# Ten conditioning pieces summed by VectorE instead of TensorE, in a two-block transformer kernel, with weight buffers given back one at a time

## The chip, the cores and the metric

The kernel runs as one program on 1 core of a Trainium2 chip. The metric is the device time of one execution in microseconds; before the change it was 2329.08 us (median of 3 runs, 2328.78 to 2331.86). The core's engines work side by side, each through its own instructions in order: TensorE (PE; PEld are its weight loads), VectorE (DVE), ScalarE (ACT), GpSimd (POOL), and SyncE (SP), which here only issues the DMAs.

## The reference, cut to what matters

Two blocks of two layers each work on 256 latent and 256 context tokens of width 1024, in fp32. Each layer is steered by adaLN parameters, a vector times a wide weight matrix, once for the latent and once for the context condition:

```
# first block, layer i
mod_lat = (silu_c @ ada_w[i] + ada_b[i])[:, None, :]      # 3 x 1024
mod_ctx = silu_cc @ ada_w[i] + ada_b[i]
# second block, layer l
sh1, sc1, g1, sh2, sc2, g2 = adaln_params(c, w_mod[l], b_mod[l])        # 6 x 1024
csh1, csc1, cg1, csh2, csc2, cg2 = adaln_params(c_ctx, w_mod[l], b_mod[l])
...
x = x + g2 * conv_ffn(hf, w_up[l], conv_w[l], w_down[l])
if not last:                      # the last layer leaves the context tokens out
    xc = xc + cg2 * conv_ffn(hcf, w_up[l], conv_w[l], w_down[l])
```

The first block has an HGRN2 layer (16 heads) and an MLA layer (16 heads); each layer of the second block has a mixer (attention, pooling, Fourier) and a conv-FFN. In the last layer of each block some of the six (or three) parameters are used for the latent tokens alone: the gate of the MLA layer, and all but the first shift and scale of the second block's layer 1.

## The kernel before, in words

**Stages.** The first block's HGRN2 layer (L0) runs to about 835 us of the span, its MLA layer (L1) to about 1120, the second block's layer 0 to about 1910, with its FFN from about 1490, and layer 1 to the end. All activations stay in SBUF; weights are streamed from HBM once.

**Products.** An fp32 product is made of three fp32r products: a matrix is split into a high part (a cast, `hi`, by ScalarE) and a low part (`lo = raw - hi`, by VectorE), and `mm3` issues hi times hi, hi times lo and lo times hi. Each weight is split so when it arrives.

**Weight stream.** `plan` lists all chunks of weights in the order of use; a chunk is at most 128 x 1024 fp32 (512 KB). `load_chunk` issues its DMA on SP's queue into one of `RAW = 3` buffers (`wraw`), `weights_hi` and `weights_lo` split it into one of `HL = 4` pairs of buffers (`whi`, `wlo`). The raw buffer is free after the low part is made, and its next DMA is issued then; the pair is free when the whole work item that used it is done:

```
for r in it.run(w):
    ...
freed[0] += it.n
```

**Order.** Work items stand in strings written by hand (`L0_ORDER`, `L1_ORDER`, `MIX1`, `MIX2`, `FFN`); in `FFN`, `v` and `g` are up products (one chunk each), `d` and `e` the two down products (each 9 items; an item has one chunk of two row blocks, `d5` and `d7` half a chunk, `d8` four chunks), and `A` takes the next adaLN item. Chains of small operations (norms, attention heads, evictions) run as generators between the items; a clock kept while the program is built decides where their instructions go.

**adaLN pieces.** A piece is 512 columns of one parameter matrix; it has four items (256 rows, one chunk). `ada_one` multiplies both conditions at once: the stationary tile `condc` holds four columns (latent and context, hi and lo), the moving tile the weight's hi and lo parts, four matmuls of 512 columns per item. `fin` then copies the 4 x 512 result, transposes it with four small matmuls and adds the bias. In all there are 36 pieces.

**Masks.** `k_lvl` (level masks of HGRN2) and `k_band` (window mask) come as fp32 and VectorE casts them to bytes.

**L1's first items.** `c` projects keys and values of all four token tiles (2, 3, 0, 1), `a` the queries, `z` gates, `q` and `k` open a group of heads.

Of the kernel before, what the change touches and what calls it, by code (L numbers as in the profile page):

```python
# [29 lines left out]
def shape_constants():  # L30
# [11 lines left out]
    c["k_lvl"] = m  # L42
# [12 lines left out]
    c["k_band"] = np.stack([bad[0:128, 128:256], bad[128:256, 0:128]], 1).astype(f32)  # L55
# [26 lines left out]
def tile_two_blocks(ctx: ExitStack, tc: tile.TileContext, I, out: bass.AP):  # L82
# [48 lines left out]
    def note(kind, op, a, k):  # L131
# [22 lines left out]
        "c a z1 q0 k0 z0 z2 q1 k1 z3 o1 x q2 k2 o0 z5 q3 k3 z4 o2 o3 z6 z7 o4 o5 o6 o7")  # L154
# [5 lines left out]
    MIX2 = (  # L160
        "A A a0 A g02 g03 a2 g04 A g05 a4 g06 g07 a6",
        "a0 g03 g02 a2 g04 g07 A g05 a4 g06 a6 A")
    FFN = (
# [150 lines left out]
    plan, loaded, raws, parts_of = [], [], {}, {}  # L314
    freed = [0]
# [7 lines left out]
    n_first = 16  # L323

    def place(name, dt, j, n_set, n):
        if j < n_first:
            return first_pool[0].tile([P, 1024], dt, tag="s" + name, name="s" + name, bufs=n_set)
        return wp.tile([P, 1024], dt, tag="w" + name, name="w" + name, bufs=n)

    def load_chunks(j, after):  # L330

        while len(loaded) < len(plan) and (len(loaded) <= j + SRAW if len(loaded) < n_first
                                           else len(loaded) <= max(j, n_first - 1) + RAW):
            load_chunk(len(loaded), after)

    def load_chunk(j, after):
        loaded.append(j)
        raw = place("raw", F32, j, SRAW, RAW)
# [8 lines left out]
    def weights_hi():  # L347
        for j, (parts, fn, need) in enumerate(plan):
            yield cond(lambda: j in raws and j < freed[0] + (HL if j >= n_first else SHL))
# [4 lines left out]
            if isinstance(fn, tuple):  # L354
                parts_of[j] = fn[0](raw)
            else:
                m, n = raw.shape[1], fn or parts[0].shape[1]
                hi = place("hi", F32R, j, SHL, HL)
                act.copy(hi[:, :m], raw)
                parts_of[j] = hi[:, :m], n  # L360
            tell(("whi", j))

    def weights_lo():
        for j, (parts, fn, need) in enumerate(plan):
            yield has(("whi", j))
            raw = raws.pop(j)
            if isinstance(fn, tuple):
                parts_of[j] = fn[1](raw, parts_of[j])
            else:
                hi, n = parts_of[j]  # L370
                m = hi.shape[1]
                lo = place("lo", F32R, j, SHL, HL)
# [3 lines left out]
            load_chunks(j, last[0])  # L376

    class Item:
# [4 lines left out]
        def __init__(self, run, chunks=(), need=None, first=None):  # L383
            self.run, self.need, self.chunks, self.start = run, need, chunks, first or len(chunks)

    def register(items):

        for it in items:
            it.first, it.n = len(plan), len(it.chunks)
            plan.extend(c if isinstance(c, tuple) else (c, None, None) for c in it.chunks)  # L390

    def run_items(items):
        for it in items:
            if it.need is not None:
                until(it.need)
            w = []
# [7 lines left out]
            last[0] = 0.0  # L404
# [7 lines left out]
            freed[0] += it.n  # L412
# [8 lines left out]
    def mm3(ps, ops, start=True, stop=True, every=0):  # L421
# [80 lines left out]

    def cond_split(cname, ccname):

        st = const.tile([P, KD, 4], F32R, tag="cond" + cname, name="cond" + cname)
        for j, nm in enumerate((cname, ccname)):
            sg = small("cs_s", 8)
# [18 lines left out]
    def ada_one(w, cname, bias, b0, mname, j, k2):  # L526
# [4 lines left out]
        def fin():  # L531
            r = sp.tile([4, 512], F32, tag="ada_r", name="ada_r", bufs=1)
# [1506 lines left out]
```

## Time and profile before

| | value |
|---|---|
| median of 3 runs | 2329.08 us |
| time of the profiled execution | 2327.35 us |
| its span (first to last instruction) | 2325.3 us |
| mean granted TensorE clock | 0.984 of full speed |
| busy: TensorE | 2225.0 us (96%) |
| busy: VectorE | 1669.0 us (72%) |
| busy: ScalarE | 1124.3 us (48%) |
| DMA, mean over the span | 125 GB/s, 290.63 MB |

Busy time is the union of an engine's instructions. A matmul's own duration is longer than the distance to the next one, since they overlap in the array; what a matmul costs is read from the distance between starts. A row's bracket says how long the engine had been idle before it and what ended that.

### The profile page before, as it was taken

The page shows a single profiled execution, that of the slowest core. Times are in us where ns is not written, and L with a number is a line of the kernel's source. Part 1 is how long each engine was busy: PE and PEld are TensorE (multiplying, and loading weights), DVE is VectorE, ACT ScalarE, POOL GpSimd, SP SyncE. Part 2 cuts the span into 40 slices and gives each one's busy share as a digit, 9 for nine tenths or more (in the row PEclk, how much of TensorE's full clock was granted, in tenths as well). Part 3 has the DMA queues.
Part 4 walks back from the last instruction along what each step waited for, and adds up shares of the span by engine and source line. Part 5 has one row for each costly group of instructions (what it writes and reads, how often), then busy time and mean ns, then how long its engine had stood idle before and what let it go on. Part 6 is the DMA issues. An engine that isn't in the chain of part 4 may idle for free.

```text
span 2325.3 us, 33917 instructions
## 1 busy us (share of the span) xinstructions
PE 2225.0 (96%) x13051; PEld 1893.0 (81%) x13051; DVE 1669.0 (72%) x3016; ACT 1124.3 (48%) x1963; POOL 35.8 (2%) x38
## 2 busy tenths in 40 slices
PE   5999999999999987999899999999999999998998
PEld 3888888888888877889788878876777878997987
DVE  6677867776778777888757854688746646876977
ACT  7344444443445345565445533466523335655644
POOL 0000000000000000000000000100010010000000
PEclk8999999999999998999999999999999999998999
DMA  7223324332434223233422344267643234455664
GB/s 254 68 73 110 108 91 119 99 109 91 127 100 127 92 91 90 81 106 126 147 83 90 100 136 127 64 208 217 207 156 109 91 93 127 136 164 153 195 192 140
DMA packets 324043, 290.63 MB, mean 125 GB/s; under 512 B 10562, under 2 KB 257706, under 8 KB 323882
## 3 DMA queue, kind: packets, MB, share of 16 engines
q1 hardware_dynamic: 323881, 288.47, 40.3%
q8 instruction: 103, 1.69, 0.3%
q14 instruction: 59, 0.48, 0.1%
HBM read 287.34 MB, written 1.09 MB: 124 GB/s over the span
## 4 chain that ended last, share of the span: by engine, by line
PE 86%; DVE 6%; ACT 2%; DMA 2%; issue 1%; SPq 0%; DVEq 0%; ACTq 0%
PE psmm L195 64%; PE pssm L195 19%; PE pssm L201 3%; DVE wlo L180 2%; ACT whi L180 1%; DMA wraw<-in_w_mod_dram 0%; DMA wraw<-in_w_in_dram 0%; DVE x L180 0%; DMA wraw<-in_w_out_dram 0%; ACT pssm L180 0%; DVE rs_t L180 0%; DVE PT L180 0%; DMA wraw<-in_w_down_dram 0%; DVE b_st L180 0%; DVE rt L180 0%
## 5 line engine op out<-in xcount | busy, mean ns | idle before, releaser
L180 DVE TENSOR_TENSOR wlo<-wraw,whi 128x1024 fp32r<-128x1024 f32 (+1 forms) x504 | 607.8, 1218 | 185.2 <-ACT whi L180 178.9
L180 ACT CAST whi<-wraw 128x1024 fp32r<-128x1024 f32 (+1 forms) x504 | 519.3, 1040 | 388.8 <-PE psmm L195 275.1
L195 PE MATMUL psmm<-hhi,whi 128*128 128x512 f32 (+1 forms) x1832 | 651.0, 355 | 4.8 <-ACT hhi L180 2.3
L195 PE MATMUL psmm<-hhi,wlo 128*128 128x512 f32 (+1 forms) x1832 | 634.5, 346 | 13.1 <-DVE wlo L180 13.1
L195 PE MATMUL psmm<-hlo,whi 128*128 128x512 f32 (+1 forms) x1832 | 633.1, 346 | 5.0 <-DVE hlo L180 5.0
L195 PEld LDWEIGHTS psmm<-hhi,wlo 128*128 128x128 f32 x1832 | 350.4, 191 | 58.3 <-DVE wlo L180 15.3
L195 PEld LDWEIGHTS psmm<-hhi,whi 128*128 128x128 f32 x1832 | 350.5, 191 | 48.5 <-ACT whi L180 3.1
L195 PEld LDWEIGHTS psmm<-hlo,whi 128*128 128x128 f32 x1832 | 350.0, 191 | 42.2 <-DVE hlo L180 5.8
L180 DVE TENSOR_TENSOR X<-X,Tn 128x512 f32<-128x512 f32 x192 | 123.9, 687 | 56.6 <-PE pssm L195 29.0
L195 PE MATMUL psmm<-whi,yh 128*128 128x512 f32 x412 | 163.7, 397 | 0.4 <-ACT yh L180 0.4
L195 PE MATMUL psmm<-wlo,yh 128*128 128x512 f32 x412 | 160.8, 390 | 0.1
L195 PE MATMUL psmm<-whi,yl 128*128 128x512 f32 x412 | 160.7, 390 | 0.0
L195 PE MATMUL psmm<-wlo,hhi 128*128 128x256 f32 x464 | 132.9, 286 | 5.4 <-DVE wlo L180 5.4
L195 PE MATMUL psmm<-whi,hhi 128*128 128x256 f32 x464 | 136.8, 295 | 1.3 <-ACT hhi L180 1.3
L195 PE MATMUL psmm<-whi,hlo 128*128 128x256 f32 x464 | 132.7, 286 | 0.3 <-DVE hlo L180 0.2
L195 PE MATMUL pssm<-X,Km 128*128 128x128 f32 x896 | 126.7, 285 | 1.3 <-ACT Km L180 1.3
L180 ACT COPY Km<-X 128x512 f32<-128x512 f32 x112 | 74.4, 665 | 108.4 <-DVE X L180 73.7
L195 PEld LDWEIGHTS pssm<-X,Km 128*128 128x128 f32 x896 | 119.8, 191 | 7.8 <-ACT Km L180 2.1
L180 DVE SCALAR_TENSOR_TENSOR conv<-psmm,cols,conv 128x510 f32<-128x510 f32 (+1 forms) x176 | 107.9, 613 | 24.6 <-ACT conv L180 21.5
L195 PE MATMUL pssm<-whi,condc 128*4 128x512 f32 x256 | 102.3, 399 | 0.0
L195 PE MATMUL pssm<-wlo,condc 128*4 128x512 f32 x256 | 101.1, 395 | 0.0
L195 PEld LDWEIGHTS psmm<-wlo,hhi 128*128 128x128 f32 x464 | 90.2, 194 | 6.8 <-DVE wlo L180 6.2
(345 smaller groups left out, 3312.8 us busy)
## 6 DMA issues: line engine op xcount, KB each, us to landing
wraw<-in_w_mod_dram SPq DMA_DIRECT2D x96, 512.0 KB
wraw<-in_w_up_dram SPq DMA_DIRECT2D x88, 512.0 KB
wraw<-in_hg_w_in_dram SPq DMA_DIRECT2D x80, 512.0 KB
wraw<-in_w_in_dram SPq DMA_DIRECT2D x68, 512.0 KB
wraw<-in_w_down_dram SPq DMA_DIRECT2D x40, 512.0 KB
wraw<-in_ada_w_dram SPq DMA_DIRECT2D x32, 512.0 KB
wraw<-in_mla_w_in_dram SPq DMA_DIRECT2D x20, 512.0 KB
sraw<-in_ada_w_dram SPq DMA_DIRECT2D x16, 512.0 KB
```

Source lines behind the costliest of these rows:

```text
L180: r = fn(*a, **k)
L195: pe.matmul(o, a, b, start=start, stop=stop)
L201: pe.transpose(o, i, idn)
```

## The change

Ten of the 36 adaLN pieces, those used for the latent tokens alone (`mod1` 4 and 5, `bmod1` 4 to 11), are no longer multiplied by TensorE. `ada_lat` keeps a 128 x 512 sum `ada_s`: ScalarE writes the first term (weight rows times the condition's value of that partition), VectorE adds the other seven with one scalar_tensor_tensor each, and TensorE sums over partitions with four matmuls against a column of ones. Their chunks have no hi and lo parts and count in a class of their own (`w+`), so they take no pair of buffers; they still pass through the three raw buffers. `ada_s` and the old `ada_r` share one buffer, so a piece's first term waits until the piece before it is finished (`ada_after`). The `A`s move in the strings: 56 instead of 52 in layer 0's FFN, none any more in layer 1, and in that FFN they stand beside `d` and `e`.

`release` gives a pair of buffers back within an item, as soon as its last use is issued, in the items that hold several chunks. L1's `c` is split into `c1` (token tiles 2, 3) and `c0` (0, 1), each with its own loads, with `a`, `z1` and `z0` between them, and `q` no longer waits for the keys. The level loop of an HGRN2 head starts after that of the head before it (`lvl`). Both masks arrive as bytes.

```
-    L1_ORDER = ("c a z1 q0 k0 z0 z2 q1 k1 z3 o1 x q2 k2 o0 z5 q3 k3 z4 o2 o3 z6 z7 o4 o5 o6 o7")
+    L1_ORDER = ("c1 a z1 z0 c0 z2 q0 k0 q1 k1 z3 o1 x q2 k2 o0 z5 q3 k3 z4 o2 o3 z6 z7 o4 o5 o6 o7")
     FFN = (
-        "U g1 v2 A A g2 A A v3 A A A g3 A A v4 g4 A A v5 A A g5 ... v12 A A g12 A A d0 A d1 A d2 A d3 A d4 A A A d5 A "
-        "d6 d7 A d8 v13 g13 ... v21 g21 e0 e1 e2 e3 e4 e5 e6 e7 e8",
+        "U g1 v2 A g2 A v3 A g3 A v4 A g4 ... v12 A g12 A A A d0 A A d1 A A d2 A A d3 A A d4 A A d5 A A d6 A A d7 A A d8 A A "
+        "v13 g13 ... v21 g21 e0 A A e1 A A e2 A A e3 A A e4 A A e5 A A e6 A A e7 e8",
...
+    def ada_lat(w, cname, bias, b0, mname, j, k2):
+        key = (mname, j)
+        free = ada_after(key)
+        def hi(raw):
+            if k2 == 0:
+                ada_open[key] = sp.tile([P, 512], F32, tag="ada_r", name="ada_s", bufs=1)
+                act.activation(ada_open[key], raw[:, :512], AF.Copy, scale=cfull[cname][:, 0:1])
+            return ada_open[key]
+        def lo(raw, acc):
+            for i in range(2):
+                k = 2 * k2 + i
+                if k:
+                    dve.scalar_tensor_tensor(acc, raw[:, i * 512:(i + 1) * 512], cfull[cname][:, k:k + 1], acc,
+                                             ALU.mult, ALU.add)
+            return [acc]
+        def fin(acc):
+            ps = bank("sm")
+            for b in range(4):
+                mm(ps[:, b:b + 1], acc[:, b * P:(b + 1) * P], st.one[:, 0:1], True, True)
...
+        return Item(run, [([rows], (hi, lo), free if k2 == 0 else None)], cls="w+")
...
             mm(ps, al, bh, False, stop and i == n - 1)
+            if rel and i % rel == rel - 1 and i < n - 1:
+                release()
...
-            freed[0] += it.n
+            if not it.keep:
+                freed[it.cls] += max(0, it.n - released[0])
...
-            lvf = row4k("lvf", (P, 7, P))
-            dma(lvf, I["k_lvl"])
-            dve.tensor_copy(st.lvl, lvf.unsqueeze(2).to_broadcast([P, 7, 4, P]))
+            dma(st.lvl, I["k_lvl"])
...
-                    bandf = row2k("bandf", (P, 2, P))
-                    dma(bandf, I["k_band"])
-                    dve.tensor_copy(L.band, bandf)
+                    dma(L.band, I["k_band"])
```

What stands in a row on the engines now is shown at three places. On TensorE, in the first down product of layer 0's FFN, between items d0 and d1, before (`psmm<-w..,y..` are the down product's matmuls, `pssm<-w..,condc` an adaLN item):

```order
L195 MATMUL psmm<-whi,yh 128x512
L195 MATMUL psmm<-wlo,yh 128x512
L195 MATMUL psmm<-whi,yl 128x512
L195 MATMUL pssm<-whi,condc_905 4x512
L195 MATMUL pssm<-wlo,condc_905 4x512
L195 MATMUL pssm<-whi,condc_905 4x512
L195 MATMUL pssm<-wlo,condc_905 4x512
L195 MATMUL psmm<-whi,yh 128x512
L195 MATMUL psmm<-wlo,yh 128x512
L195 MATMUL psmm<-whi,yl 128x512
```

and on the same engine between d1 and d2 after the change (`one,ada_s` is the end of a piece):

```order
L194 MATMUL psmm<-whi,yh 128x512
L194 MATMUL psmm<-wlo,yh 128x512
L194 MATMUL psmm<-whi,yl 128x512
L194 MATMUL pssm<-one,ada_s 128x1 x4
L194 MATMUL psmm<-whi,yh 128x512
L194 MATMUL psmm<-wlo,yh 128x512
L194 MATMUL psmm<-whi,yl 128x512
```

The four matmuls of an item are gone; four one-column matmuls stand once for four items. On SP's queue, the loads of that first down product from d3 on, before (`in_w_mod` are adaLN chunks, `in_w_down` the down product's):

```order
L188 DMA wraw<-in_w_down_dram 128x2x512
L188 DMA wraw<-in_w_mod_dram 128x2x512
L188 DMA wraw<-in_w_down_dram 128x2x512
L188 DMA wraw<-in_w_mod_dram 128x2x512 x3
L188 DMA wraw<-in_w_down_dram 128x512
L188 DMA wraw<-in_w_mod_dram 128x2x512
L188 DMA wraw<-in_w_down_dram 128x2x512
L188 DMA wraw<-in_w_down_dram 128x512
L188 DMA wraw<-in_w_mod_dram 128x2x512
L188 DMA wraw<-in_w_down_dram 128x2x512 x4
L188 DMA wraw<-in_w_up_dram 128x8x128 x18
```

and after, from before d4 on:

```order
L187 DMA wraw<-in_w_mod_dram 128x2x512 x2
L187 DMA wraw<-in_w_down_dram 128x2x512
L187 DMA wraw<-in_w_mod_dram 128x2x512 x2
L187 DMA wraw<-in_w_down_dram 128x512
L187 DMA wraw<-in_w_mod_dram 128x2x512 x2
L187 DMA wraw<-in_w_down_dram 128x2x512
L187 DMA wraw<-in_w_mod_dram 128x2x512 x2
L187 DMA wraw<-in_w_down_dram 128x512
L187 DMA wraw<-in_w_mod_dram 128x2x512 x2
L187 DMA wraw<-in_w_down_dram 128x2x512 x4
L187 DMA wraw<-in_w_mod_dram 128x2x512 x2
L187 DMA wraw<-in_w_up_dram 128x8x128 x18
```

Two adaLN chunks now stand before every chunk of the down product. On TensorE at the start of L1, around the transposes of the context rows (`ident,xn`), before (the matmuls on both sides are `c`'s, whose second half needs these rows):

```order
L195 MATMUL psmm<-whi,hhi 128x256
L195 MATMUL psmm<-wlo,hhi 128x256
L195 MATMUL psmm<-whi,hlo 128x256
L201 MATMUL pssm<-ident,xn 128x128 x16
L195 MATMUL psmm<-whi,hhi 128x256
L195 MATMUL psmm<-wlo,hhi 128x256
L195 MATMUL psmm<-whi,hlo 128x256
```

and after (the matmuls are those of `z1`, which needs latent rows alone; `ident,qa_r` belongs to the queries' norm):

```order
L194 MATMUL psmm<-hlo,whi 128x256
L194 MATMUL psmm<-hhi,wlo 128x256
L200 MATMUL pssm<-ident,xn 128x128 x4
L200 MATMUL pssm<-ident,qa_r 128x128 x4
L194 MATMUL psmm<-hhi,whi 128x256
L194 MATMUL psmm<-hlo,whi 128x256
L194 MATMUL psmm<-hhi,wlo 128x256
L194 MATMUL psmm<-hhi,whi 128x256
L194 MATMUL psmm<-hlo,whi 128x256
L194 MATMUL psmm<-hhi,wlo 128x256
L200 MATMUL pssm<-ident,xn 128x128 x4
```

The transposes now stand inside products that do not need them, after 96 matmuls of `c1` and `a`.

## Rows read from the trace of the kernel before

**Rows 1.** The page: busy time (share of the span) and instructions of each engine.
```profile
PE 2225.0 (96%) x13051; PEld 1893.0 (81%) x13051; DVE 1669.0 (72%) x3016; ACT 1124.3 (48%) x1963; POOL 35.8 (2%) x38
```

**Rows 2.** Windows: stretch; busy PE, PEld, DVE, ACT, POOL; granted clock, DMA share, GB/s.
```profile
70.00:835.00 765.00, 763.66 (x4604) 653.40 (x4603) 574.86 (x1045) 333.10 (x595) 0.00 (x0) 1.00 0.33 100
835.00:960.00 125.00, 104.38 (x654) 93.26 (x652) 93.12 (x236) 66.16 (x145) 0.00 (x0) 0.92 0.32 101
...
1497.00:1698.00 201.00, 201.00 (x943) 145.81 (x942) 154.90 (x195) 116.43 (x155) 0.00 (x0) 1.00 0.64 198
1698.00:1755.00 57.00, 54.74 (x243) 41.33 (x242) 28.90 (x32) 16.76 (x20) 6.50 (x4) 1.00 0.39 124
```

**Rows 3.** Waits of TensorE over the span: total us, times, longest.
```profile
PE psmm L195 <- DVE wlo L180: 20.5, 13, 3.0
```

**Rows 4.** Timeline of TensorE: start and length; adaLN matmuls, then a piece's transposes.
```profile
1608.71 0.40 PE L195 MATMUL pssm<-whi,condc 128*4 128x512 f32 x1
...
1610.56 0.39 PE L195 MATMUL psmm<-hhi,whi 128*128 128x512 f32 x1
...
1612.05 0.41 PE L201 MATMUL pssm<-ident,ada_r 4*128 4x4 f32 x4
1612.38 0.50 PE L195 MATMUL psmm<-hhi,whi 128*128 128x512 f32 x1
```

**Rows 5.** Timeline of TensorE in L0: four fp32 matmuls of 128 columns.
```profile
152.09 1.16 PE L195 MATMUL pssm<-X,Km 128*128 128x128 f32 x8 [0.55 <-ACT Km L180]
```

**Rows 6.** Timelines of SP and ScalarE: eight loads merged; two of them and their casts.
```profile
2081.62 17.41 SPq L188 DMA_DIRECT2D wraw<-in_w_out_dram  x8
...
2084.97 0.37 SPq L188 DMA_DIRECT2D wraw<-in_w_out_dram  x1
2088.72 1.05 ACT L180 CAST whi<-wraw 128x1024 fp32r<-128x1024 f32 x1 [0.23 <-DMA wraw<-in_w_out_dram]
2098.66 0.37 SPq L188 DMA_DIRECT2D wraw<-in_w_out_dram  x1
2103.46 1.05 ACT L180 CAST whi<-wraw 128x1024 fp32r<-128x1024 f32 x1 [1.51 <-DMA wraw<-in_w_out_dram]
```

**Rows 7.** VectorE's groups by form, in the whole span: busy us, mean ns.
```profile
L180 DVE TENSOR_TENSOR X<-X,Tn 128x512 f32<-128x512 f32 x192 | 123.9, 687 | 56.6 <-PE pssm L195 29.0 <-issue 18.4 <-ACT whi L180 6.6
```

**Rows 8.** Timelines of VectorE and GpSimd around d5 to d7.
```profile
1706.86 1.22 DVE L180 TENSOR_TENSOR wlo<-wraw,whi 128x1024 fp32r<-128x1024 f32 x1
1716.95 6.50 POOL L180 TENSOR_TENSOR x<-x,rt 128x512 f32<-128x512 f32 x4 [250.51 <-DVE rt L180]
1720.22 5.46 DVE L180 TENSOR_TENSOR wlo<-wraw,whi 128x1024 fp32r<-128x1024 f32 x3 [0.23 <-ACT whi L180]
```

**Rows 9.** Timeline of TensorE: first and last of seven waits after items of several chunks.
```profile
870.73 0.58 PE L195 MATMUL psmm<-wlo,hhi 128*128 128x256 f32 x1 [2.10 <-DVE wlo L180]
...
2236.20 0.58 PE L195 MATMUL psmm<-hhi,wlo 128*128 128x256 f32 x1 [2.48 <-DVE wlo L180]
```

**Rows 10.** Timelines of VectorE and TensorE at the two masks.
```profile
57.16 3.88 DVE L180 CAST lvl<-lvf 128x3584 uint8<-128x3584 f32 x1 [0.53 <-DMA lvf<-in_k_lvl_dram]
...
61.70 0.58 PE L195 MATMUL psmm<-hlo,whi 128*128 128x256 f32 x1 [3.75 <-DVE hlo L180]
...
1125.97 0.29 DVE L180 CAST band<-bandf 128x256 uint8<-128x256 f32 x1 [3.20 <-DMA bandf<-in_k_band_dram]
...
1127.81 0.39 PE L195 MATMUL psmm<-wlo,hhi 128*128 128x256 f32 x1 [3.02 <-DVE wlo L180]
```

**Rows 11.** Timeline of TensorE: two waits at the start of L1.
```profile
885.76 0.45 PE L201 MATMUL pssm<-ident,xn 128*128 128x128 f32 x1 [5.71 <-DVE xn L180]
...
915.03 0.58 PE L195 MATMUL psmm<-whi,qaT 128*128 128x256 f32 x1 [5.02 <-ACT qaT L180]
```

**Rows 12.** Windows of 5 us after two waits of TensorE (columns as in rows 2).
```profile
885.00:890.00 5.00, 4.24 (x20) 4.12 (x21) 2.67 (x5) 3.76 (x7) 0.00 (x0) 0.50 0.00 0
...
1945.00:1950.00 5.00, 3.94 (x17) 3.64 (x18) 3.50 (x3) 2.75 (x4) 0.00 (x0) 0.56 0.43 125
```

More of the change, by code (lines that the diff above doesn't have):

```diff
@@ L321, in split, with place, gone, load_chunks @@
         dve.tensor_tensor(lo, src, hi, ALU.subtract)
[L323 to L334, printed above, removed]
+    def place(name, dt, j):
+        k = cls[j][0]
+        bufs = cap_raw[k] if name == "raw" else cap[k]
+        return (first_pool[0] if k == "s" else wp).tile([P, 1024], dt, tag=k + name, name=k + name, bufs=bufs)
+    def gone(j, after):
+        k = cls[j][0]
+        raw_gone[k].add(raw_rank[j])
+        while raw_freed[k] in raw_gone[k]:
+            raw_freed[k] += 1
+        load_chunks(after)
+    def load_chunks(after, most=10000):
+        while len(loaded) < min(len(plan), most):
+            j = len(loaded)
+            if raw_rank[j] >= raw_freed[cls[j][0]] + cap_raw[cls[j][0]]:
+                return
+            load_chunk(j, after)
     def load_chunk(j, after):
         loaded.append(j)
-        raw = place("raw", F32, j, SRAW, RAW)
+        raw = place("raw", F32, j)
         o = 0
@@ L375, in weights_lo, with release, __init__ @@
             tell(("w", j))
-            load_chunks(j, last[0])
+            gone(j, last[0])
+    released = [0]
+    def release(n=1):
+        freed[running[0].cls] += n
+        released[0] += n
     class Item:
-        def __init__(self, run, chunks=(), need=None, first=None):
+        def __init__(self, run, chunks=(), need=None, first=None, cls="w", keep=False):
             self.run, self.need, self.chunks, self.start = run, need, chunks, first or len(chunks)
+            self.cls, self.keep = cls, keep
     def register(items):
@@ L390, in register @@
             plan.extend(c if isinstance(c, tuple) else (c, None, None) for c in it.chunks)
+            for _ in it.chunks:
+                cls.append(it.cls)
+                rank.append(n_of[it.cls])
+                n_of[it.cls] += 1
+                raw_rank.append(n_raw[it.cls[0]])
+                n_raw[it.cls[0]] += 1
     def run_items(items):
@@ L403, in run_items @@
             got = take(0, it.start)
-            last[0] = 0.0
+            last[0], released[0] = 0.0, 0
             for r in it.run(w):
@@ L524, in tile_two_blocks, with ada_after, latent_only, run @@
     ada_open = {}
-    def ada_one(w, cname, bias, b0, mname, j, k2):
+    ada_prev = [None, {}]
+    def ada_after(key):
+        if key not in ada_prev[1]:
+            ada_prev[1][key] = has(*ada_prev[0] or ())
+            ada_prev[0] = (key,)
+        return ada_prev[1][key]
+    def latent_only(mname, j):
+        return (mname, j) in (("mod1", 4), ("mod1", 5)) or mname == "bmod1" and j >= 4
+    def ada_lat(w, cname, bias, b0, mname, j, k2):
[17 more added lines that the diff above has]
+                mm(ps[:, b:b + 1], acc[:, b * P:(b + 1) * P], st.one[:, 0:1], True, True)
+            clk[0] += 800
+            made[id(ps.tensor)] = (clk[0] + LAG, ps)
+            yield (ps,)
+            c = b0 + 4 * j
+            dve.tensor_tensor(mod[mname][:, 4 * j:4 * j + 4, 0], ps[:, 0:4], col[bias][:, c:c + 4], ALU.add)
+            tell(key)
+            yield
+        def run(wk):
+            if k2 == 3:
+                spawn(fin(wk[0]), (wk[0],))
+            yield 0
+        rows = w[k2 * 256:(k2 + 1) * 256, j * 512:(j + 1) * 512]
+        return Item(run, [([rows], (hi, lo), free if k2 == 0 else None)], cls="w+")
+    def ada_one(w, cname, bias, b0, mname, j, k2, kind="w"):
+        if latent_only(mname, j):
+            return ada_lat(w, cname, bias, b0, mname, j, k2)
+        free = ada_after((mname, j))
         if (mname, j) not in ada_open:
@@ L803, in run @@
                     yield from mm3(ps[:, i * 256:(i + 1) * 256],
-                                   [(h[0][:, k, t], h[1][:, k, t]) + wk[k] for k in range(KD)], every=2)
+                                   [(h[0][:, k, t], h[1][:, k, t]) + wk[k] for k in range(KD)], every=2,
+                                   rel=4 * (t2 == i == 1))
                     yield 0
@@ L814, in hgrn @@
         l0 = st.l0
+        if hd:
+            yield has(("lvl", hd - 1))
         x, qs = st.X[hd], st.q[hd]
@@ L855, in hgrn @@
             yield (x, Km)
+        tell(("lvl", hd), 0.0)
         if hd:
@@ L1189, in run @@
                                [(wk[k][0][:, m], wk[k][1][:, m], h[0][:, k, 256:], h[1][:, k, 256:])
-                                for k in range(KD)], every=2)
+                                for k in range(KD)], every=2, rel=4 * j)
                 yield 0
@@ L1365, in kv @@
             ps = bank("mm")
-            yield from mm3(ps[:, :256], [(h[0][:, k, t], h[1][:, k, t]) + w[k] for k in range(KD)], every=2)
+            yield from mm3(ps[:, :256], [(h[0][:, k, t], h[1][:, k, t]) + w[k] for k in range(KD)], every=2,
+                           rel=4 * (tk == kv_order[-1]))
+            if tk == kv_order[-1]:
+                release()
             vs = ps[:, 128:256].rearrange("p (a b) -> p a b", a=2)
@@ L1379, in q @@
             ps = bank("mm")
-            yield from mm3(ps[:, :256], [(h[0][:, k, t], h[1][:, k, t]) + w[k] for k in range(KD)], every=2)
+            yield from mm3(ps[:, :256], [(h[0][:, k, t], h[1][:, k, t]) + w[k] for k in range(KD)], every=2,
+                           rel=4 * (c == 1 and tk == 3))
             d = L.qrow[:, tk - tb, c * 256:(c + 1) * 256]
@@ L1390, in b2_items @@
         all_h = has(*[(hkey, tk) for tk in tks])
+        kv_order = (2, 3, 0, 1) if last else tks
         def kv_q0():
@@ L1395, in run @@
                 h = hT[hk]
-                for tk in (2, 3, 0, 1) if last else tks:
+                for tk in kv_order:
                     yield has((hkey, tk))
@@ L1941, in tile_two_blocks @@
         first_pool.append(su)
-        for j in range(6):
-            load_chunk(j, 1.0)
+        load_chunks(1.0, 6)
         xs = [x_in(tk) for tk in range(4)]
-        load_chunks(-1, 1.0)
+        load_chunks(1.0)
         for gen in supply:
```

93 lines of the change are left out of this document (57 added, 36 removed), and 13 rows, old and new, of tables (FFN, MIX1).

## The prediction

> **What bounds the kernel now.** The first view is the page's busy times: TensorE works 2225.0 of 2325.3 us, the next engine, VectorE, 1669.0 [rows 1]. The share is an average, so the second view is the windows by stage: in L0 TensorE is busy 763.66 of 765 us and in the up products of layer 0's FFN 201.00 of 201, where VectorE has its fullest stage with 154.90 [rows 2]. There, whatever TensorE no longer does shortens the span, unless something else gets late. The other 100.3 us (2325.3 - 2225.0) are waits, mostly at the borders of stages, so the third view is the list of what TensorE waited for: 20.5 us in 13 waits for the low part of a weight [rows 3]. The sum below is made against the profiled execution's 2327.35 us; the median is 1.7 us more, and I state the result for the median.
>
> **The matmuls removed.** Ten pieces of four items of four matmuls are 160. Eight adaLN matmuls stand between 1608.71 and 1610.56, 0.231 us each [rows 4]; their own 0.40 us overlap and are not the price. 160 x 0.231 = **-37.0 us**: 8 items in L0 (7.4), 28 in layer 0's FFN (25.9), 4 in layer 1 (3.7); those 4 now stand in layer 0's FFN, without matmuls. The Trainium skill (TensorE: Matmul & The Clock Gate, "Back-to-back issue gap") gives about 131 ns as the sustained distance of matmuls with 512 columns. The rows differ, 231 ns for fp32r here, and decide; by the page's figure the same 160 would be an estimated 21 us.
>
> **The end of a piece.** Before, four transposes: 0.33 us between 1612.05 and 1612.38 [rows 4]. Now four fp32 matmuls of one column, which this trace does not have. Bounds: no more than the transposes, or as much as four fp32 matmuls of 128 columns, 1.16 us [rows 5], so 0 to +8 us for ten. One column is nearer to the transposes' four: **+2**.
>
> **VectorE and ScalarE.** 70 scalar_tensor_tensor of 128 x 512 replace 40 low parts of 1.22 us [rows 8]. With the 0.69 us of an operation of that size with two SBUF inputs [rows 7] that is 48 us for 49: nothing. ScalarE loses 40 casts of 1.05 us [rows 6] for 10 activations. Neither is the bound, so 0; the cover is TensorE's full row, and what it costs without that cover is the next term.
>
> **The loads beside the down products.** Here something gets late. The pieces' chunks take no hi/lo pair, but all chunks go through three raw buffers, and now two adaLN chunks stand before each down chunk. Three chunks per group, three buffers: each buffer is used once per group, and the slowest sets the pace, that of the down chunk, which is held for landing, cast, low part and hand-over. From issue to cast a load took 3.75 us (2084.97 to 2088.72) and 4.80 (2098.66 to 2103.46) [rows 6]; with 1.05, 1.22 and about 0.2 that is 6.2 to 7.3 us per use. The eight loads merged say the same for a stretch where supply is short: (17.41 - 0.37) / 7 = 2.43 us per chunk, 7.3 for three. I take a landing of 4.6, so 7.05. TensorE needs 24 x 0.231 = 5.5 us for a full item and 2.8 for a half (d5, d7). So a full group is 1.6 short, a full chunk after a half item 4.2 (7.05 - 2.8), and a half chunk (about 5.3) is in time. The first term of a piece also waits for the end of the piece before it, which stands behind d1, d3, d5, d7, and everything behind it in the chain of casts waits too, so little is fetched ahead: d2 is 0.8 late, d3 and d4 1.6 each, d6 and d8 4.2 each, and the fourth chunk of d8, whose first pass uses a chunk every six matmuls (1.4 us), 2.9: 15 us. The second down product starts with more in hand, since 18 up chunks without adaLN stand before it: e4 1.6, e6 4.1, e8 2.4, together 8. **+23**. Before, TensorE lost 2.3 of 57 us in the first down product [rows 2], behind d8, which the next term counts. Lower bound: 6.2 per group, +8. Upper: 7.3 per group (+28), and VectorE beside GpSimd's four additions after d5: three low parts take 5.46 us there, not 3 x 1.22 = 3.7 [rows 8], and if all eight sums near them double (0.69 each, in two down products) that is 9 more: +37.
>
> A rule speaks against this place: by the Trainium skill (SBUF — State Buffer, "Who interferes with whom") a VectorE instruction with two SBUF inputs contends with a GpSimd instruction that reads SBUF, and the later one blocks. The trace agrees for the low part, 5.46 us for three; the new sums have two SBUF inputs as well. Without the rule the upper bound would be +28.
>
> While supply is late TensorE idles. After its wait of 5.71 us the granted clock was 0.50 for 5 us, the lower of the two levels [rows 12], 2.5 us of work lost; three of the new waits exceed 4 us: **+4** (0 to +8).
>
> **Buffers given back singly.** Seven times TensorE waits 2.0 to 2.7 us, 16.2 in all, for the first low part after an item that held four chunks [rows 9]: its cast could start only when the whole item was done. Now three of the four pairs are free up to a few microseconds earlier, and a cast and a low part need 2.3. I take **-15** (-8 to -16), and **-3** (0 to -6) for the clock behind two of them, 0.56 in one window [rows 12].
>
> **Masks.** The cast of the level mask holds VectorE for 3.88 us ahead of the last low parts of the first norm, and TensorE waits 3.75 for these; the window mask's cast waits 3.20 for its DMA, and TensorE then 3.02 for a weight behind it [rows 10]. Both casts are gone and the loads are no longer in VectorE's row: **-8**, with 1.3 for the low clock after the first (-3 to -9).
>
> **The start of L1.** TensorE is busy 104.38 of 125 us at a clock of 0.92 [rows 2]. It waits 5.71 us for the context rows and 5.02 for the queries' norm [rows 11]. `a`, `z1`, `z0` now cover the first and `z1`, `z0`, `c0`, `z2` the second; that is 10.7 us and up to 5 of clock (0.50 behind the first, rows 12). Against it, `z0` and `z2` no longer fill the gaps of the first heads, `c0` loads two chunks again, and ten chunks in some 28 us are near the 2.43 us per chunk of rows 6. **-10** (-16 to +3).
>
> The wait between two heads' level loops: 0 (0 to +4), hidden by L0's products [rows 2]; should it not be hidden, `f` of the head after next is late.
>
> **Sum.** -37 + 2 + 23 + 4 - 15 - 3 - 8 - 10 = -44: 2283 for a profiled execution, **2285** for the median.
>
> **The rivals.**
> *The loads keep up.* With 309 GB/s at full share (198 / 0.64, rows 2) a group's 1.57 MB need 5.1 us, less than 5.5. Against it rows 6, where the three buffers, not the engines, set 2.43 us. With the lower bound and no clock lost: 2285 - 15 - 4 = 2266. Chance 0.15.
> *Supply at the upper bound*, the contention with GpSimd included: 2285 + 14 + 4 = 2303. Rows 8 speak for it; against it, only 4 additions per down product are on GpSimd. 0.13.
> *L1 gives nothing*, as the first heads, bare of fillers, wait for VectorE (93.12 of 125 us): 2295. 0.09.
> *Slower.* A load landing in 8.2 us instead of 4.6 would do it: each group then costs 3.7 us more, and over 12 late groups (d2 to d8, e4 to e8) 44 are gone; from 10.7 us per group the kernel is slower than 2329, at 11 near 2334. No row has a landing over 4.80. 0.02.
> *Nothing is gained*: TensorE is covered less than it seems and waits elsewhere for what it saved, about 2329. Against it 201.00 of 201 us. 0.02.
>
> **Numbers.** The forecast has 0.59, 0.41 the others. The own range of each term makes the forecast 2274 to 2296; taking in most of both supply rivals and L1's gives 2263 to 2304, with about 2 in 10 outside. A measurement of this kernel tells 0.2% (4.7 us) from no change. Faster 0.95, same 0.02, slower 0.03.
>
> **What would show it.** No `condc` matmuls in the second half of layer 0's FFN and about 160 fewer; waits of TensorE for low parts of 1 to 4 us before d3, d4, d6, d8, e4, e6, with loads of down chunks about 7 us apart; no wait of 2 us or more after d8, e8 or `k`; no cast of `lvl`; no wait of 5 us between c1 and the first heads. The forecast is wrong by 15 or more if down chunks come every 5.5 us, by as much the other way if every 8, and by 10 if L1 still has its two waits.

## The result and the profile after

The changed kernel takes **2303.68 us** (median of 4 runs, 2302.68 to 2304.82) against 2329.14 (median of 4): 0.9888 of the time before, 95% interval 0.9871 to 0.9905. Run once more beside other kernels it took 2306.00 against 2327.25, 0.9911 (0.9886 to 0.9935). So it is faster, as forecast, but by 21 to 25 us (about 1%) where 44 were predicted; 2303.68 is 18.7 more than the forecast and 0.3 us below the upper end of its range. The profiled execution took 2304.82 us, its span is 2302.8, 22.5 less than before.

The page's busy times after (before: [rows 1]):

```profile
PE 2199.0 (95%) x12931; PEld 1886.3 (82%) x12931; DVE 1673.4 (73%) x3035; ACT 1084.9 (47%) x1915; POOL 36.9 (2%) x38
```

TensorE is busy 26.0 us less, and its idle time grew from 100.3 to 103.8 (2302.8 - 2199.0). It has 120 instructions fewer: 160 `condc` matmuls and 40 transposes went, 80 records of one column came (each of the 40 one-column fp32 matmuls stands as two). The list of what TensorE waited for, total, times and longest, after (before: [rows 3]):

```profile
PE pssm L200 <- DVE xn L179: 14.9, 5, 7.1
PE psmm L194 <- DVE wlo L179: 11.8, 13, 4.6
...
PE psmm L194 <- DVE hlo L179: 6.8, 5, 2.8
PE pssm L194 <- DVE PT L179: 6.8, 4, 3.7
PE psmm L194 <- DVE rp L179: 5.4, 1, 5.4
...
PE pssm L194 <- DVE ada_s L179: 3.3, 1, 3.3
```

The 20.5 us for low parts fell to 11.8, although most of those 11.8 are new, beside the down products. `PT` and `rp` are chains of the attention heads in L1 that did not stand among the large waits before, and `ada_s` is the end of a piece.

Where the 22.5 us lie is read by comparing the start of the same instruction in both timelines:

| instruction | before | after | difference | of this stage | predicted |
|---|---|---|---|---|---|
| first matmul of the last head's output product, end of L0 | 823.92 | 809.62 | -14.3 | -14.3 | -12 |
| first `vv` cast, end of L1 | 1124.71 | 1119.34 | -5.4 | **+8.9** | -13 |
| first `rt` of the mixer's residual, block 2, layer 0 | 1459.64 | 1450.57 | -9.1 | -3.7 | -5 |
| last `rt` for the context rows, end of layer 0's FFN | 1911.77 | 1910.26 | -1.5 | **+7.6** | -2 |
| last `rt` of layer 1 | 2316.59 | 2294.05 | -22.5 | -21.0 | -12 |

The last column distributes the terms of the prediction over the stages (the matmuls by their items, the returned buffers by where the seven waits stood, the masks at the start and with -3 in the third row). L0 is near; L1 grew by 8.9 us where it should have shrunk by 13, layer 0's FFN lost more than all its 28 items gave, and layer 1 gained more than expected.

Windows after, of L1, of the two down products and of layer 1 (columns as in [rows 2]):

```profile
825.00:1100.00 275.00, 244.51 (x1581) 219.36 (x1581) 214.12 (x479) 151.65 (x312) 0.00 (x0) 0.94 0.35 106
...
1660.00:1725.00 65.00, 56.92 (x233) 44.53 (x232) 39.55 (x50) 12.51 (x14) 5.99 (x4) 0.89 0.68 218
...
1850.00:1910.00 60.00, 51.83 (x235) 41.59 (x233) 38.07 (x56) 21.20 (x37) 6.45 (x4) 0.94 0.48 152
1910.00:2302.00 392.00, 369.68 (x2738) 350.93 (x2738) 309.65 (x578) 215.10 (x378) 15.20 (x14) 0.98 0.54 162
```

and the windows of L1 and of layer 1 before:

```profile
840.00:1103.00 263.00, 238.23 (x1564) 215.03 (x1563) 208.50 (x471) 146.56 (x303) 0.00 (x0) 0.96 0.33 103
...
1912.00:2325.00 413.00, 382.33 (x2770) 359.63 (x2769) 315.80 (x585) 221.35 (x385) 13.32 (x14) 0.96 0.52 160
```

In layer 1 TensorE idled 30.7 us before (413 - 382.33) and 22.3 after, and the granted clock went from 0.96 to 0.98, worth another 8.7 us (413 x 0.04 less 392 x 0.02); with 3.7 for four items that is the 21. In the first down product it now idles 8.1 of 65 us at a clock of 0.89, in the second 8.2 of 60 at 0.94.

### The profile page after: what moved, and what is told of

Its sections match the earlier page's. It is cut to its first block, busy times and chain, and to the rows that moved or that the text cites. A ratio compares the mean times of both kernels' runs of the same rounds, so it can differ in the third digit from the quotient of the medians.

```text
span 2302.8 us, 33643 instructions
## 1 busy us (share of the span) xinstructions
PE 2199.0 (95%) x12931; PEld 1886.3 (82%) x12931; DVE 1673.4 (73%) x3035; ACT 1084.9 (47%) x1915; POOL 36.9 (2%) x38
## 4 chain that ended last, share of the span: by engine, by line
PE 85%; DVE 7%; DMA 3%; ACT 3%; issue 1%; SPq 0%; ACTq 0%; DVEq 0%
PE psmm L194 64%; PE pssm L194 18%; PE pssm L200 3%; DVE wlo L179 2%; DMA wraw<-in_w_down_dram 1%; ACT whi L179 1%; ACT pssm L179 1%; DMA wraw<-in_w_up_dram 1%; DVE hlo L179 0%; DVE ada_s L179 0%; DVE b_st L179 0%; DVE rs_t L179 0%; DVE x L179 0%; DVE nh_t L179 0%; DMA wraw<-in_hg_w_in_dram 0%
## 5 line engine op out<-in xcount | busy, mean ns | idle before, releaser
L179 DVE TENSOR_TENSOR wlo<-wraw,whi 128x1024 fp32r<-128x1024 f32 x466 | 563.4, 1216 | 194.7 <-ACT whi L179 192.1
L179 ACT CAST whi<-wraw 128x1024 fp32r<-128x1024 f32 x466 | 481.5, 1039 | 456.4 <-PE psmm L194 309.3
L194 PEld LDWEIGHTS psmm<-wlo,yh 128*128 128x128 f32 x412 | 78.7, 191 | 27.6 <-DVE wlo L179 13.3
L194 PEld LDWEIGHTS psmm<-whi,yh 128*128 128x128 f32 x412 | 78.7, 191 | 21.6 <-ACT whi L179 4.8
L194 PEld LDWEIGHTS psmm<-whi,yl 128*128 128x128 f32 x412 | 78.6, 191 | 17.1 <-DVE yl L179 0.4
```

Source lines behind the costliest of these rows:

```text
L179: r = fn(*a, **k)
L194: pe.matmul(o, a, b, start=start, stop=stop)
```

## The experiments

All runs beside the kernel before on the same chip; "of before" is the ratio that the text compares, since chips differ by a few us.

| run | median us | of before | 95% interval |
|---|---|---|---|
| changed kernel | 2303.68 | 0.9888 | 0.9871 to 0.9905 |
| after_again | 2306.00 | 0.9911 | 0.9886 to 0.9935 |
| l1_exact | 2303.22 | 0.9896 | 0.9881 to 0.9910 |
| l1_gates_back | 2301.06 | 0.9883 | 0.9866 to 0.9899 |
| before_l1 | 2332.58 | 1.0025 | 1.0013 to 1.0036 |
| spread | 2278.92 | 0.9790 | 0.9775 to 0.9804 |
| no_release | 2323.52 | 0.9984 | 0.9971 to 0.9997 |
| on_tensore | 2317.42 | 0.9960 | 0.9948 to 0.9972 |
| adds_dve | 2305.28 | 0.9911 | 0.9885 to 0.9937 |
| half_sums | 2298.05 | 0.9872 | 0.9853 to 0.9890 |
| half_bytes | 2292.16 | 0.9848 | 0.9832 to 0.9864 |
| spread_l1 | 2275.12 | 0.9775 | 0.9757 to 0.9793 |
| spread_z2 | 2277.76 | 0.9775 | 0.9760 to 0.9790 |

**The changed kernel again.** No edit. 

> The changed kernel unaltered, beside the other runs on the same chip, since chips differ by some us: 0.989 of the kernel before, about 2300 to 2304.

 It took 2306.00, a little above that, 0.9911. Two measurements of one kernel thus differ by 0.0023; differences below that are not read as effects.

**The start of L1 undone.** In order and dependences (`l1_exact`; the products of `c` and `a` are still issued in steps, between which small operations can stand): the order, one item `c` for all four token tiles, and `q` behind the keys:

```
-        "c1 a z1 z0 c0 z2 q0 k0 q1 k1 z3 o1 x ...")
+        "c a z1 q0 k0 z0 z2 q1 k1 z3 o1 x ...")
-            for tk in (2 * s, 2 * s + 1):
+            for tk in (2, 3, 0, 1):
-        return Item(run, cut(...), has("qa", *need))
+        return Item(run, cut(...), has("kv", "qa", *need))
```

> The changed kernel with L1 as it was before: keys of all four token tiles in one item, gates z0 and z2 behind the first group of heads, q waits for the keys again. The prediction as it stood (the new start of L1 saves 10 us) expects 2314. The reading of the trace after (from the last norm of L0 to the last attention head the changed kernel takes 11 us longer than the kernel before) expects 2293, with the waits of 5.7 and 5.0 us for context rows and queries back and the waits inside the heads gone.

 And in part (`l1_gates_back`), keys apart, the gates back among the heads:

```
-        "c1 a z1 z0 c0 z2 q0 k0 q1 k1 z3 o1 x ...")
+        "c1 a z1 c0 q0 k0 z0 z2 q1 k1 z3 o1 x ...")
```

> The changed kernel with the keys still apart (c1, a, z1, c0), but z0 and z2 behind the first group of heads as before. Theory 1 (the heads lose what the gates no longer fill): 2288 to 2296, the waits of the first two groups of heads gone, though a wait of 4 to 6 us ahead of the first group may stay. Rival (splitting the keys, with its chunks loaded twice, is what costs): 2302 to 2306, no change against the changed kernel.

 They take 2303.22 and 2301.06, no difference that can be told. So neither the gain nor the loss that I expected came; the number is near the rival of `l1_gates_back`, but its reason, the split keys, is not it, since `l1_exact` has no split keys. The waits moved as expected, though: in `l1_exact` 6.2 us for the context rows and 5.5 for the queries are back, those for `rp` and `PT` are gone. L1, measured as in the table above, is 307.0 us (810.48 to 1117.47) and 306.7 (810.22 to 1116.94), where the changed kernel has 309.7 and the kernel before 300.8. So the order costs at most some 3 us here, and about 6 of the 8.9 are not in the order.

**The start of L1 alone, in the kernel before.** The edits of L1 and nothing else. 

> The kernel before with the change of L1 alone (keys apart, z1 and z0 between them, z2 ahead of the heads, q waits for the queries only; no other part of the change). The prediction's term expects 10 us less than before. The first reading of the trace after (this start costs 11) expects 11 more. What the two runs that put the order back showed (no difference that can be told) expects within 4 us of the kernel before.

 It is slower by 0.25% (0.13 to 0.36%), 5.8 us, little more than two measurements of one kernel differ by, and its L1 takes 307.1 us (823.83 to 1130.97), 6.3 more than before. Waits of TensorE in L1 in the changed kernel:

```profile
854.07 3.76 PE L200 MATMUL pssm<-ident,xn 128*128 128x128 f32 x16 [4.19 <-DVE xn L179]
...
910.92 0.77 PE L194 MATMUL psmm<-qaT,whi 128*128 128x256 f32 x2 [5.37 <-DVE rp L179]
...
940.87 2.71 PE L194 MATMUL pssm<-PT,kvR 128*128 128x256 f32 x11 [3.67 <-DVE PT L179]
...
998.97 0.51 PE L194 MATMUL pssm<-ol,wv 128*128 128x256 f32 x2 [2.01 <-DVE ol L179]
```

and in the kernel before with this start alone:

```profile
916.33 0.39 PE L195 MATMUL psmm<-wlo,qaT 128*128 128x256 f32 x1 [0.41 <-DVE wlo L180]
...
924.57 0.47 PE L195 MATMUL psmm<-qaT,whi 128*128 128x256 f32 x2 [4.78 <-DVE rp L180]
...
953.15 2.71 PE L195 MATMUL pssm<-PT,kvR 128*128 128x256 f32 x11 [4.16 <-DVE PT L180]
```

The two waits of [rows 11] are gone from their places: nothing of 5.7 us ahead of the context rows, 0.41 at the first product with `qaT`. But 8 us after that TensorE waits 4.78 for `rp` (the rotated queries), then 4.16 for `PT`, and smaller ones follow: the chain of the first heads runs on VectorE, and `z0` and `z2`, which stood there before, are used up. The same two waits, 5.37 and 3.67, stand in the changed kernel. Windows of L1 (columns as in [rows 2]) in the changed kernel and in `l1_exact`:

```profile
809.60:1119.30 309.70, 279.21 (x1768) 248.89 (x1766) 240.23 (x526) 168.61 (x344) 0.00 (x0) 0.95 0.35 105
...
810.50:1117.50 307.00, 276.32 (x1767) 247.35 (x1766) 237.88 (x524) 167.62 (x343) 0.00 (x0) 0.95 0.33 103
```

and in the kernel before and in `before_l1`:

```profile
823.90:1124.70 300.80, 274.37 (x1762) 245.92 (x1760) 236.15 (x521) 166.78 (x342) 0.00 (x0) 0.97 0.34 106
...
823.80:1131.00 307.20, 272.94 (x1762) 243.30 (x1760) 238.37 (x523) 169.10 (x345) 0.00 (x0) 0.98 0.36 107
```

TensorE idles 30.5 us in the changed kernel's L1 (309.70 - 279.21) and 30.7 with the start undone; in the kernel before it is 26.4, and 34.3 with the new start.

**The items spread.** The 24 items on TensorE two behind each of `v2` to `g7`, the 32 sums one behind each of `v8` to `g12`, `v13` to `g21` and `e0` to `e3`, none beside `d`:

```
-        "... v12 A g12 A A A d0 A A d1 A A ... d8 A A v13 g13 ... v21 g21 e0 A A e1 A A ... e7 e8",
+        "... v7 A A g7 A A v8 A g8 A ... v12 A g12 A d0 d1 ... d8 v13 A g13 A ... v21 A g21 A e0 A e1 A e2 A e3 A e4 ... e8",
```

> The changed kernel with the 56 adaLN items of layer 0's FFN in other places: the 24 on TensorE two behind each of v2 to g7, the 32 sums one behind each of v8 to g12, v13 to g21 and e0 to e3; none beside d. Theory 1 (three raw buffers cannot feed two adaLN chunks and a down chunk in 5.5 us, but one adaLN chunk and an up chunk they can): the losses in the two down products, about 15 us of waits and about 9 of lower clock, go, 2277 to 2284. Rival (the up products, where VectorE has its fullest stage, now wait as much): 2295 to 2306. A wait ahead of the second norm, if the last pieces come too late, would show after e8.

 2278.92, 0.979 of before: 23 to 28 us less than the changed kernel by the two measurements of it. Layer 0's FFN takes 432.26 us (1449.43 to 1881.69), where the changed kernel has 459.69 (1450.57 to 1910.26): 27.4. Windows of spread at the places of the two down products:

```profile
1660.00:1725.00 65.00, 65.00 (x288) 53.84 (x287) 25.89 (x31) 11.84 (x13) 6.88 (x4) 1.00 0.35 110
1840.00:1881.00 41.00, 41.00 (x196) 34.30 (x194) 20.94 (x38) 16.65 (x30) 6.89 (x4) 1.00 0.27 81
```

TensorE never waits there and the clock is full. The rival, a wait moved to the up products, did not come: between 1485 and 1880 TensorE's list of waits holds 0.7 us once and 0.4 once.

**Buffers given back at the end of an item.**

```
     def release(n=1):
-        freed[running[0].cls] += n
-        released[0] += n
+        return
```

> The changed kernel with pairs of weight buffers given back only at the end of an item, as before. The prediction's term (seven waits of 2.0 to 2.7 us and clock) expects 18 us more, 2322. The reading of the trace after (the waits behind k, d8 and e8 of layer 1 are gone, 6.7 us, but behind two items a wait of 2.5 and 2.8 us for a norm's low part stands in the same place) expects 8 to 10 more, 2312 to 2314. Rival (the waits went because the order around them moved): 2304 to 2306.

 2323.52, 0.9984: 17 to 22 us more, the prediction's own term (18) and not the smaller one that I read from the trace afterwards. In the timeline of TensorE without the release stand, in the places of [rows 9]:

```profile
1154.82 0.50 PE L194 MATMUL psmm<-hhi,wlo 128*128 128x512 f32 x1 [2.04 <-DVE wlo L179]
...
1487.70 0.58 PE L194 MATMUL psmm<-hhi,wlo 128*128 128x256 f32 x1 [2.07 <-DVE wlo L179]
...
1742.10 0.50 PE L194 MATMUL psmm<-hhi,wlo 128*128 128x512 f32 x1 [2.19 <-DVE wlo L179]
...
1920.93 0.58 PE L194 MATMUL psmm<-hhi,wlo 128*128 128x256 f32 x1 [2.44 <-DVE wlo L179]
...
2231.87 0.58 PE L194 MATMUL psmm<-hhi,wlo 128*128 128x256 f32 x1 [2.48 <-DVE wlo L179]
```

and with it, the changed kernel, two waits of the same size on another releaser:

```profile
1481.77 0.58 PE L194 MATMUL psmm<-hlo,whi 128*128 128x256 f32 x1 [2.48 <-DVE hlo L179]
...
1913.29 0.38 PE L194 MATMUL psmm<-hlo,whi 128*128 128x256 f32 x1 [2.79 <-DVE hlo L179]
```

There the next item's activations are late (`hlo`), so the free buffer gives nothing at once. That the release is still worth 17 to 22 comes from smaller waits and the clock: for low parts TensorE waits 25.0 us in 23 waits without it, 11.8 in 13 with it. In the two profiled executions its idle time is 116.6 us (2322.9 - 2206.3) against 103.8, and it is busy 7.3 us longer with the same instructions, at a mean granted clock of 0.977 against 0.980.

**The pieces back on TensorE**, at the places of the change.

```
     def latent_only(mname, j):
-        return (mname, j) in (("mod1", 4), ("mod1", 5)) or mname == "bmod1" and j >= 4
+        return False
```

> The changed kernel with the ten pieces multiplied by TensorE again, all items at the places of the change, two beside each down item. 160 matmuls come back (37 us), the ends of ten pieces get some 5 us cheaper, and the loss beside the down products, 27 us by the run with the items spread, goes for the most part, since a group of two adaLN items and a down item then takes TensorE 7.4 us and the buffers 7.3: 10 to 16 more than the changed kernel, 2311 to 2319. Rival (the four pairs of buffers now set the pace and the loss stays): 30 to 37 more, 2332 to 2340.

 2317.42, on the chip where the changed kernel took 2306.00: +11.4, in the expected interval. Beside the down products (1650 to 1905) its longest wait for a low part is 1.4 us. So summing on VectorE at these places is worth 11 us, of the 37 that the matmuls cost.

**GpSimd's additions on VectorE.**

```
-                            (dve if hf else pool).tensor_tensor(x, x, r, ALU.add)
+                            dve.tensor_tensor(x, x, r, ALU.add)
```

> The changed kernel with the twelve additions of the residual that GpSimd does in the down products moved to VectorE. Theory (VectorE's instructions with two SBUF inputs are stretched beside GpSimd's, 0.75 to 1.3 to 1.8 us, and the down chunks' low parts come later for it): 2 to 6 less than the changed kernel. Rival (the loads through three buffers set the pace alone): within 1.5 us of it, or slower by the added work of VectorE.

 2305.28, 0.9911, against 0.9911: no difference, the rival. (The edit moves 18 additions, the 12 of the down products and 6 of the mixers.) That the two engines hinder each other shows; rows of GpSimd and VectorE in the changed kernel:

```profile
1694.86 3.49 POOL L179 TENSOR_TENSOR x<-x,rt 128x512 f32<-128x512 f32 x2 [2.01 <-DVE rt L179]
...
1695.30 1.92 DVE L179 TENSOR_TENSOR wlo<-wraw,whi 128x1024 fp32r<-128x1024 f32 x1
...
1697.21 1.69 DVE L179 SCALAR_TENSOR_TENSOR ada_s<-wraw,cfc,ada_s 128x512 f32<-128x512 f32 x1
```

and d6's low part in `adds_dve`, where GpSimd does nothing beside it:

```profile
1692.97 1.22 DVE L179 TENSOR_TENSOR wlo<-wraw,whi 128x1024 fp32r<-128x1024 f32 x1
```

The low part takes 1.92 us where it has 1.22 without GpSimd, the sum 1.69 for 0.75. But the additions cost VectorE 0.69 each when it does them itself, about as much as it is hindered. So the run puts one load on VectorE's row in the place of another; it does not show what that row would cost with neither.

**What sets the pace beside the down products.** Half of the sums left out; VectorE then adds only the second half of each adaLN chunk:

```
             for i in range(2):
                 k = 2 * k2 + i
-                if k:
+                if i:
```

> The changed kernel with half of the sums left out (of each adaLN chunk that VectorE sums, only the second half is added, so VectorE does 40 instead of 70 sums); the chunks are loaded whole. Theory 1 (the three raw buffers, each held from the issue of a load through its landing, cast and low part, set the pace beside the down products): 0 to 5 less than the changed kernel. Rival A (VectorE, which has the sums ahead of the down chunks' low parts, sets it): 10 to 20 less.

 And the same with half of the bytes left out: the latent pieces' chunks are 128 rows instead of 256:

```
-        rows = w[k2 * 256:(k2 + 1) * 256, j * 512:(j + 1) * 512]
+        rows = w[k2 * 256:k2 * 256 + P, j * 512:(j + 1) * 512]
```

> As the run with half of the sums, and the latent pieces' chunks are loaded with half of their bytes (128 instead of 256 weight rows each, so that part of the weights is left out of the sum). Theory 1: the landing is the longest part of a buffer's use, 3.7 to 7.1 us of about 7, and two of three chunks become half as large: 8 to 18 less than the changed kernel. Rival A (VectorE alone): no more than the run with half of the sums gives. Rival B (landing is a fixed latency, not a matter of bytes): no difference to the run with half of the sums, both near the changed kernel.

 They take 0.9872 and 0.9848 of before: 4 to 9 and 9 to 15 us less than the changed kernel; spread gives 23 to 28. The first lies between Theory 1 and Rival A, the second inside Theory 1's interval. Neither resource alone is the answer: half of VectorE's sums is worth some 6, half of the bytes as much again (2298.05 and 2292.16 on one chip, their runs apart), and about half of the loss stays. For the most part that is one wait. Between 1650 and 1885 of `half_bytes` TensorE waits 8.4 us for low parts and 1.0 for high ones, and 5.20 of them are one wait, before item e6; ScalarE's, VectorE's and TensorE's rows there:

```profile
1851.02 1.05 ACT L179 CAST whi<-wraw 128x1024 fp32r<-128x1024 f32 x1 [0.78 <-DMA wraw<-in_w_down_dram]
...
1855.81 1.97 DVE L179 TENSOR_TENSOR wlo<-wraw,whi 128x1024 fp32r<-128x1024 f32 x1
...
1857.83 0.80 PE L194 MATMUL psmm<-wlo,yh 128*128 128x512 f32 x1 [5.20 <-DVE wlo L179]
```

The chunk has long landed; its low part begins 3.7 us after its high part is done, since two sums (1.38 and 1.63 us beside GpSimd's additions) and two residual products stand ahead of it on VectorE. The same wait is 4.58 us in the changed kernel, 5.22 in `half_sums` and 5.24 in `adds_dve`; `spread`, with no sums there, does not have it. A run with a fourth raw buffer, which would test the buffers directly, was not made.

**A better version.** Spread with the gates back (`spread_l1`: the two edits above together) and with `z0` ahead but `z2` behind (`spread_z2`, order `c1 a z1 z0 c0 q0 k0 z2 q1 k1`). 

> The spread items together with the order c1, a, z1, c0 and the gates z0 and z2 behind the first group of heads. If the two are independent: what spread alone gave, 0.979 of the kernel before, and 0 to 3 us less. If the gates' place is worth something once the rest runs free: 0.976 to 0.978.

 

> The spread items, and of the gates only z0 ahead of the second half of the keys, z2 behind the first group of heads (order c1, a, z1, z0, c0, q0, k0, z2). If z0 covers the wait for the context rows (6 us in the run with both gates behind the heads) and z2 alone is enough for the heads: 2 to 5 us less than spread with both gates behind. If every gate that covers the one wait is missing at the other: within 2 us of it, 0.976 to 0.979 of the kernel before.

 Both take 0.9775 of before, 2275.12 and 2277.76, the fastest here, though their intervals overlap that of spread alone. In `spread_z2` the wait for `rp` in L1 is 7.2 us: a gate that covers one wait is missing at the other.

## Why the prediction was right in direction and 19 us off

That the time lies inside the stated range is luck: it is 0.3 us from its end, the second measurement (0.9911) would be 2308 on the median before, outside, and the range reached that far for rivals that did not come. The rival *Supply at the upper bound* has the same 2303, but the supply loss was as large as forecast; the miss is elsewhere, in L1.

**The matmuls removed (-37): held.** Layer 0's FFN in spread, where nothing else gets late, is 19.9 us shorter than before (452.13 to 432.26): 25.9 of matmuls for its 28 items, less some 4 for the ends of its pieces (eight of 0.81 us more, seven of 0.33 fewer; the remaining 2 us I did not trace); L0 became 8.9 us shorter behind its first level masks, for 7.4.

**The end of a piece (+2): mis-sized, +5.** Between two down matmuls of the changed kernel:

```profile
1681.65 0.95 PE L194 MATMUL pssm<-one,ada_s 128*128 128x1 f32 x8
1682.46 0.49 PE L194 MATMUL psmm<-whi,yh 128*128 128x512 f32 x1
```

0.81 us where the transposes took 0.33: ten times 0.5. One column does not make an fp32 matmul short: its eight records follow each other at about 0.11 us, at a granted clock of 1.00.

**The loads beside the down products (+23, clock +4): held in the sum.** 27.4 by spread. But two errors cancel in it: 16.3 us of idle time in the two windows where I had 23, and 10.8 of clock (65 x 0.11 and 60 x 0.06) where I had 4, outside its own 0 to 8. The waits stand where I put them: 2.1 us before d3 (1.33 + 0.76; forecast 1.6), 3.9 before d6 (3.31 + 0.54; 4.2), 1.8 before e4 (1.07 + 0.76; 1.6), 5.8 before e6 (1.17 + 4.58; 4.1). But there is none before d4 (1.6), and in d8 they come to 1.5 (0.74 + 0.45 + 0.26) where I had 7.1. The loads and casts of down chunks, and TensorE's waits, in the changed kernel:

```profile
1666.52 0.37 SPq L187 DMA_DIRECT2D wraw<-in_w_down_dram  x1
...
1672.29 1.04 ACT L179 CAST whi<-wraw 128x1024 fp32r<-128x1024 f32 x1 [5.38 <-DMA wraw<-in_w_down_dram]
...
1673.38 0.50 PE L194 MATMUL psmm<-whi,yh 128*128 128x512 f32 x1 [1.33 <-ACT whi L179]
...
1674.62 0.37 SPq L187 DMA_DIRECT2D wraw<-in_w_down_dram  x1
...
1686.35 0.37 SPq L187 DMA_DIRECT2D wraw<-in_w_down_dram  x1
...
1693.42 1.04 ACT L179 CAST whi<-wraw 128x1024 fp32r<-128x1024 f32 x1 [9.08 <-DMA wraw<-in_w_down_dram]
...
1694.23 1.86 PE L194 MATMUL pssm<-one,ada_s 128*128 128x1 f32 x8 [3.31 <-DVE ada_s L179]
...
1695.30 1.92 DVE L179 TENSOR_TENSOR wlo<-wraw,whi 128x1024 fp32r<-128x1024 f32 x1
...
1866.69 1.04 ACT L179 CAST whi<-wraw 128x1024 fp32r<-128x1024 f32 x1 [2.20 <-DMA wraw<-in_w_down_dram]
...
1870.84 1.97 DVE L179 TENSOR_TENSOR wlo<-wraw,whi 128x1024 fp32r<-128x1024 f32 x1
...
1872.87 0.80 PE L194 MATMUL psmm<-wlo,yh 128*128 128x512 f32 x1 [4.58 <-DVE wlo L179]
```

The chunks of d3 and d4 are issued 8.1 us apart (d5's half chunk, at 1680.60, is left out here), and from issue to cast a full chunk takes 3.7 to 7.1 us, where I took 4.6 for all. (That no row has a landing over 4.80 was true only of the two that I picked: another of the eight merged loads of [rows 6] was issued at 2089.24 and cast at 2095.00. And the rival *Slower* at 11 us per group sums to 2332, not 2334.) The 3.31 us are put down to the last sum of a piece, whose end stands ahead of d6 on TensorE; but d6's own high part was ready only at 1694.46 and its low part at 1697.22, so that without the sum TensorE would have stood there as well. After it the granted clock was low (0.50 from 1695 to 1700, the lower of its two levels), and the eight records take 1.86 us instead of 0.95. The 4.58 us before e6 are no load: the high part was done at 1867.73, and the low part began 3.1 us later, behind three sums and two residual products on VectorE, whose own row I had put at nothing. The forecast's lower bound ("the loads keep up") is refuted by spread. Of the upper bound by contention this one wait is a part, and how much is open: with GpSimd's additions on VectorE it is 5.24.

**Buffers given back singly (-15, clock -3): held**, 17 to 22 by no_release, though by other waits than the seven alone.

**The masks (-8): held** as far as the trace tells: the start of L0 is 5.4 us earlier (82.38 to 77.02 at the first `Km` product), and the 3.02 us at the window mask became 0.61.

**The start of L1 (-10): this step failed, and it is most of the miss.** In the kernel before it costs 5.8 us (3.0 to 8.4) instead of saving 10, and in the changed kernel undoing it changes nothing that can be told. I counted two waits as covered, and both did go from their places; I saw that the heads lose their fillers, and let the first outweigh the second. In the changed kernel the sum of the two is the same in either order, 30.5 and 30.7 us of idle time: what TensorE has to fill in until the first heads are through is the same list of items, and it waits for VectorE's chain either early or late. That reading of the two numbers is argued; in the kernel before, the new start adds 7.9 us of idle time, so it does not hold everywhere. The rival "L1 gives nothing, as the first heads, bare of fillers, wait for VectorE" named the mechanism, with 0.09, and was still 6 us too kind to the kernel before.

**What stays open.** With the order of L1 undone (`l1_exact`), L1 is still 6.2 us longer than before. 4.2 us of wait for the first normalized rows stand in every variant of the changed kernel but one, where the kernel before waits 1.50, with L1's start alone 1.51. The release is not the cause (without it the wait is 6.11), nor is L1's own start, nor the sums on VectorE (with the pieces back on TensorE it is 4.19); the order of L0's items is the same in both kernels. VectorE's rows ahead of that norm, in the changed kernel:

```profile
850.00 0.69 DVE L179 TENSOR_TENSOR x<-x,gt 128x512 f32<-128x512 f32 x1 [1.10 <-ACT pssm L179]
...
851.20 0.15 DVE L179 TENSOR_TENSOR sums<-sums 128x2 f32<-128x2 f32 x1
```

and before:

```profile
860.78 1.28 DVE L180 TENSOR_TENSOR x<-x,psmm 128x512 f32<-128x512 f32 x2
...
861.98 0.15 DVE L180 TENSOR_TENSOR sums<-sums 128x2 f32<-128x2 f32 x1
```

The norm's `sums` now stand behind a gate product, which waited 1.10 us for ScalarE, and one more addition, and before they did not: the order of the small operations on VectorE is another. Which edit moved it, the wait between the level loops (`lvl`) or one that shifts the planner's clock, was not tried. The terms as measured, -37, +5, +27, -20, -8 and +6, give -27, near the 21 to 25. The +6 is L1's start in the kernel before; in the changed kernel its order gives nothing and some 6 us of L1 stand there for a reason not found, so the agreement of the sum does not show what these 6 are.

## What to carry to other kernels

Work taken off the engine that sets the time must not put its loads where that engine has short items: count the chunks per item against the buffers before choosing the place; here the 32 chunks of the sums cost 27 us two at a time beside the down items, and nothing that shows one at a time, 28 of them beside the up items. Look also at the row of the engine that took the work over: a weight's low part that stands behind its new instructions is late however early the weight landed. When an item is moved to cover one wait, look up which wait it covered where it stood; if both wait for the same chain, moving it may gain nothing. And a buffer that is free a few microseconds earlier was worth more here than the long waits that it ended, since small waits and low clock went with them.

## What was not expected of the hardware

A matmul of one fp32 column against a 128 x 128 operand costs 0.20 us (0.81 for four), nearly as much as one of 512 fp32r columns (0.231 in [rows 4]). And the granted clock took two fifths of the supply loss: 10.8 of 27 us, after waits of 1.3 to 4.6 us.
